# An expert layer with product keys: the first 128 tokens by gathered rows on VectorE, the other 384 by dense blocks summed in six PSUM banks

## The chip, the cores and the metric

The kernel runs on one core of a Trainium2 chip. Times are device microseconds (us) of one launch, 512 tokens of width 1024 in float32. The time before is 4912.36 us, the median of three runs (4911.04 to 4912.63).

## The reference, cut to what matters

The kernel computes the forward pass of two blocks. The first has two mixers and then the layer below, in which each token takes 8 x 16 = 128 of 16384 experts; the second has feed-forward layers and other mixers. The change touches the expert layer alone.

```python
PEER_HEADS = 8; PEER_KEYS = 128; PEER_TOPK = 16; PEER_BLOCK = 128   # D_MODEL = 1024
def peer(h, wq, subkeys, u_tab, v_tab):
    def block(hb):                                          # 128 tokens
        q = (hb @ wq).reshape(PEER_BLOCK, PEER_HEADS, 2, 128)
        s = jnp.einsum('thsd,snd->thsn', q, subkeys)
        s1, i1 = lax.top_k(s[:, :, 0], PEER_TOPK)
        s2, i2 = lax.top_k(s[:, :, 1], PEER_TOPK)
        cand = (s1[..., :, None] + s2[..., None, :]).reshape(PEER_BLOCK, PEER_HEADS, 256)
        sc, ci = lax.top_k(cand, PEER_TOPK)
        e1 = jnp.take_along_axis(i1, ci // PEER_TOPK, axis=-1)
        e2 = jnp.take_along_axis(i2, ci % PEER_TOPK, axis=-1)
        idx = e1 * PEER_KEYS + e2
        gate = jax.nn.softmax(sc, axis=-1)
        act = jax.nn.gelu(jnp.einsum('td,thkd->thk', hb, u_tab[idx])) * gate
        return jnp.einsum('thk,thkd->td', act, v_tab[idx])
```

`u_tab` and `v_tab` are 16384 x 1024, 64 MB each. All matrix products in the kernel are made exact in float32 by three products of halves: an operand x is split as x = H + L (ACT casts H, a second engine subtracts to get L), and one product is HH, HL and LH (`mm3`, L297 to L301).

## The kernel before, in words

The layer works on all experts for all tokens. The tables are cut into 128 blocks of 128 experts (a block has one e1 and all e2). Its three stages follow each other on TensorE:

1. **Queries** (`peer_select`, `dense` with `wq`): q for 512 tokens, scores against the keys (L1098), and the first choice of 16 (L1102 to L1106), in V and I, token-major.
2. **Select**: `routing` is a generator of 156 steps (`STEPS`), and three of them are issued beside each block of U activations of the first `NU` = 56 blocks (`peer_act`). For each of four groups t of 128 tokens, seven steps are `topk` (the choice among 256 pairs, on VectorE; POOL makes the candidates and one multiply, L1187; TensorE transposes the result to `eT`). Then 32 steps build the table of gates: for each token two one-hot tiles of 128 x 128 (the row with the gate on VectorE, L1140; the other on POOL, VectorE or ACT, L1138) and one matmul of them (L1141) into `sa`, copied by ACT to `W`; a block of 32 tokens goes to DRAM as 2 MB (`WD`, 16 of them). The activations of those 56 blocks go to DRAM as `geD`.
3. **Dense**: `peer_dense` takes the blocks in groups of J = 4. 14 groups have their activations in DRAM ("spilled"), 18 make them on the spot ("fresh"); a table `order` mixes the two. For a block: 24 matmuls of U with 512 columns (fresh groups alone; `xH`, `xL` are the activations' names in the trace, `wd` and `we` the weights'), gelu, times the gates (L1233), split into `pGH` and `pGL`, V split into `pVH` and `pVL`, then 8 tiles of 128 channels x 3 matmuls with V stationary and 512 tokens of G moving, into a bank `mm`. After four blocks each of the eight sums is added from PSUM to `pacc` by VectorE (L1256). In the last group the residual r is updated (L1260), the last three channel tiles by halves of the tokens, and the sums of squares for the norm follow it (`Stat`, L2110 to L2149; squares on ACT, their sum on POOL, L2120). The first matmul of the next feed-forward layer (L299 `mm<-xH,weH`) needs that norm.

DMA queues: weights, W, ge and tables all go by SP's queue; POOL issues only a few loads in the stages before. `self.wp` holds the raw weights (`wraw`, two buffers of two blocks each). Pools give a new tile when the last use of the buffer has ended; a scheduler orders each engine's instructions.

Of the kernel before, what the change touches and what calls it, by code (L numbers as in the profile page):

```python
# [9 lines left out]
F32 = mybir.dt.float32  # L10
# [9 lines left out]
T = 512  # L20
# [10 lines left out]
STEPS = 4 * (7 + 32)     # of the routing  # L31
# [48 lines left out]
# the order in which the projections' tiles are taken: per SSD group xs, xs, B, C and z, z;  # L80
# then Hyena's parts v, x1, x2 by slabs of 256 channels, x2 behind by two slabs
# [14 lines left out]
def prep(inp):  # L96
# [33 lines left out]
    # constants that depend on shapes alone  # L130
# [4 lines left out]
    # Hyena  # L135
# [5 lines left out]
    a['pv'] = i['peer_v'][0].reshape(128, 128, 1024)  # L141
# [5 lines left out]
def hy_consts(a, i):  # L147
# [3 lines left out]
    for arg in ((2 * f.T + 1) * (2 * t.T), (2 * f.T + 1) * (2 * t.T + 1), (2 * f + 1) * (2 * t)):  # L151
        # rows (256) on partitions in 2 tiles, columns [cos 256 | sin 256]
# [16 lines left out]
    dec = np.exp(-tt * deltas).astype(f32) * f32(1.0 / 512)     # with the inverse transform's factor  # L169
    # time tiles: even 0,1 then odd 0,1; per slab of 256 channels  # L170
# [4 lines left out]
    # [64][slab][order][dir][256]  # L175
# [21 lines left out]
    # even mixer: qk, v, o, rg_x, rg_g; the gates' inputs apart  # L197
# [23 lines left out]
    # odd mixer: low-rank inputs, then r, k, v by pairs of heads; v, q, k, og of the other  # L221
# [20 lines left out]
    # block of 64, its causal part, and for each level of the inverse the lower left of a pair of blocks  # L242
# [6 lines left out]
# ---------------------------------------------------------------- kernel  # L249
class Kern:  # L250
    def __init__(self, ctx, tc, ap, at, dbg=None):
# [12 lines left out]
        # le: [s, l] s<=l ; ge ; gt ; lt  # L264
# [18 lines left out]
    # PSUM tags: mm (dense), sa, sb (small)  # L283
# [3 lines left out]
    def split(self, pool, x, name, shape=None, bufs=1, l_eng=None):  # L287
        """exact halves of x in float32r: x = H + L"""
# [33 lines left out]
    def wsplit(self, raw, l_eng=None):  # L322
        """halves of weights: every third in xp, where that is open"""
# [13 lines left out]
    def dense_steps(self, src, first, n, kt, movs, evac, chunks=None, g=128, head=0, tail=0, last=None, l_eng=None, early=(0, 0)):  # L337
        """dense, tile by tile"""
# [55 lines left out]
    def softplus(self, pool, x, out, tmpname, p, n):  # L394
        """out = max(x,0) + log1p(exp(-|x|)), by the atanh series"""
# [7 lines left out]
        nc.vector.tensor_mul(e, e, r)            # s = e / (2 + e)  # L403
        nc.vector.tensor_mul(r, e, e)            # s^2
# [15 lines left out]
        # a first guess from the halved exponent, then Newton's steps  # L420
# [7 lines left out]
    def col_bcast(self, out, col, n):  # L428
        """out[m, c*128 + t] = col[t, c] for every m"""
# [14 lines left out]
    def mod_steps(self, *sixths):  # L444
        """sixths of shift1, scale1, gate1, shift2, scale2, gate2, a quarter of one at a step"""
# [44 lines left out]
        # running sums in the chunk, what is left of it, and the whole  # L490
# [30 lines left out]
    def row_bcast(self, dst, src, r, n, rep):  # L521
        """dst[j*rep + i] = src[r + j] for i < rep, j < n (src in DRAM)"""
# [4 lines left out]
    def conv(self, tp, ps, n, taps, bias, name, bufs=3):  # L527
        """centred depthwise convolution of a PSUM tile"""
# [19 lines left out]
    def ssd_states(self, g, tp, R, got, out):  # L548
        """a group's convolved projections -> x times dt, token-major, and the states before each chunk: nine steps"""
# [12 lines left out]
        # both ways through the chunks of the sequence  # L562
# [25 lines left out]
    def ssd_heads(self, g, tp, R, got, xd, S, out):  # L588
        """a group's outputs before the gate -> two tiles; nine steps"""
# [51 lines left out]
    def ssd_gate(self, g, tp, y, z):  # L641
        """group_rmsnorm(y * silu(z))"""
# [19 lines left out]
    def ssd(self, tp, fl, fc, mod):  # L662
# [27 lines left out]
        # a group's heads beside the next one's states, projections between  # L690
# [387 lines left out]
    def peer_select(self, f2):  # L1078
# [5 lines left out]
        with self.tc.tile_pool(name='pk', bufs=1, reuse_waits='tile') as pk:  # L1084
# [31 lines left out]
            for _ in steps:  # L1116
                pass
# [1117 lines left out]
```

## Time and profile before

| what | us |
|---|---|
| median of three runs | 4912.36 |
| span of the profiled execution | 4912.9 |
| its TensorE busy | 4731.6 |
| Select: 1026.0 to 1553.0 | 527.0 |
| Dense: 1553.0 to 2627.0 | 1074.0 |
| last matmul with V to the next layer's first matmul | 6.0 |

The profiled execution's span agrees with the median of the runs within 0.6 us, so differences within the trace can be set against the runs directly. The two stages are 1601 us of it; what lies ahead and behind is not touched, apart from the seam at each end.

### The profile page before, as it was taken

The numbers are of one execution on the slowest core, as the hardware profiler recorded it, in microseconds if no ns is written. First come the engines' busy times: TensorE is split into PE (matmuls) and PEld (weight loads), VectorE is DVE, ScalarE is ACT, GpSimd is POOL, SyncE is SP. The second block draws the span as 40 slices with busy tenths as digits, with TensorE's granted clock in tenths as the row PEclk, the third lists the DMA queues.
The fourth block names the chain that finished last, engine by engine and source line by source line (L and its number), as shares of the span: only waits on it lengthen the run. The fifth ranks groups of instructions, "written<-read, shape, count | busy, mean of one in ns | idle before, by whom it ended". The sixth has DMA issues, their size and how long they took to land.

```text
span 4912.9 us, 60507 instructions
## 1 busy us (share of the span) xinstructions
PE 4731.6 (96%) x23772; PEld 3883.8 (79%) x23772; DVE 2691.2 (55%) x5211; ACT 1736.9 (35%) x2642; POOL 733.5 (15%) x694
## 2 busy tenths in 40 slices
PE   8888999998999999999999999999999999999998
PEld 4776778867888888888888888688888887778887
DVE  5775577699554545555555336663343356645333
ACT  3533222335664222322223225532232233333222
POOL 3232332355441000000001002010020020001001
PEclk9998999999999999999999999999999999998999
DMA  6232423234445444344342222222222220011322
GB/s 213 85 109 94 144 108 125 104 120 151 165 178 184 151 132 146 131 149 150 129 137 86 95 92 78 80 77 95 97 92 95 93 97 8 26 44 44 103 100 72
DMA packets 206873, 537.51 MB, mean 109 GB/s; under 512 B 11555, under 2 KB 79411, under 8 KB 199676
## 3 DMA queue, kind: packets, MB, share of 16 engines
q1 hardware_dynamic: 205084, 526.29, 31.5%
q0 software_dynamic: 1504, 7.34, 0.4%
q8 instruction: 188, 3.08, 0.3%
q14 instruction: 97, 0.79, 0.1%
HBM read 468.50 MB, written 65.09 MB: 109 GB/s over the span
## 4 chain that ended last, share of the span: by engine, by line
PE 72%; issue 13%; DVE 9%; POOL 2%; ACT 2%; DMA 2%; SPq 0%; ACTq 0%; POOLq 0%; DVEq 0%
PE mm L300 20%; PE mm L301 20%; PE mm L299 20%; PE sa L1141 2%; DMA ssee<-csD 2%; DVE oh L1140 1%; PE sa L453 1%; POOL oh L1138 1%; DVE wdL L294 1%; PE sb L2161 0%; PE sa L431 0%; POOL xL L2211 0%; PE sb L1842 0%; PE sa L1842 0%; PE sb L1849 0%
## 5 line engine op out<-in xcount | busy, mean ns | idle before, releaser
L299 PE MATMUL mm<-xH,wdH 128*128 128x512 f32 (+2 forms) x2660 | 1019.3, 385 | 9.4 <-DVE cacc L539 7.8
L301 PE MATMUL mm<-xH,wdL 128*128 128x512 f32 (+2 forms) x2660 | 1014.0, 382 | 7.4 <-DVE wdL L294 7.2
L300 PE MATMUL mm<-xL,wdH 128*128 128x512 f32 (+2 forms) x2660 | 1015.7, 382 | 2.7 <-POOL xL L2211 1.5
L293 ACT CAST wdH<-wraw 128x1024 fp32r<-128x1024 f32 (+2 forms) x382 | 394.6, 1035 | 1165.9 <-PE mm L300 833.3
L294 DVE TENSOR_TENSOR wdL<-wraw,wdH 128x1024 fp32r<-128x1024 f32 (+2 forms) x346 | 424.3, 1226 | 457.1 <-ACT wdH L293 444.4
L299 PEld LDWEIGHTS mm<-xH,wdH 128*128 128x128 f32 (+1 forms) x2660 | 505.8, 191 | 106.2 <-issue 12.5
L301 PEld LDWEIGHTS mm<-xH,wdL 128*128 128x128 f32 (+1 forms) x2660 | 506.9, 191 | 102.7 <-DVE wdL L294 10.2
L300 PEld LDWEIGHTS mm<-xL,wdH 128*128 128x128 f32 (+1 forms) x2660 | 507.0, 191 | 95.9 <-POOL xL L2211 3.3
L299 PE MATMUL mm<-xH,weH 128*128 128x512 f32 (+2 forms) x1048 | 400.7, 382 | 1.1 <-ACT xH L2209 1.1
L300 PE MATMUL mm<-pGL,pVH 128*128 128x512 f32 (+1 forms) x1036 | 401.4, 390 | 0.0
L300 PE MATMUL mm<-xL,weH 128*128 128x512 f32 (+2 forms) x1048 | 399.4, 381 | 1.0 <-POOL xL L2211 0.9
L299 PE MATMUL mm<-pGH,pVH 128*128 128x512 f32 (+1 forms) x1036 | 399.3, 387 | 0.0
L301 PE MATMUL mm<-pGH,pVL 128*128 128x512 f32 (+1 forms) x1036 | 399.3, 388 | 0.0
L301 PE MATMUL mm<-xH,weL 128*128 128x512 f32 (+2 forms) x1048 | 397.1, 379 | 0.4 <-POOL weL L294 0.3
L293 ACT CAST weH<-wraw 128x1024 fp32r<-128x1024 f32 (+2 forms) x162 | 168.2, 1038 | 469.4 <-PE mm L300 327.8
L294 DVE TENSOR_TENSOR weL<-wraw,weH 128x1024 fp32r<-128x1024 f32 (+1 forms) x155 | 190.0, 1226 | 230.9 <-ACT weH L293 205.2
L293 ACT CAST pVH<-wraw 128x1024 fp32r<-128x1024 f32 x128 | 133.0, 1052 | 486.6 <-PE mm L300 295.4
L1256 DVE TENSOR_TENSOR pacc<-pacc,mm 128x512 f32<-128x512 f32 (+1 forms) x251 | 166.7, 678 | 179.5 <-PE mm L301 179.2
L294 DVE TENSOR_TENSOR pVL<-wraw,pVH 128x1024 fp32r<-128x1024 f32 x128 | 155.2, 1223 | 179.6 <-ACT pVH L293 179.5
L300 PEld LDWEIGHTS mm<-pGL,pVH 128*128 128x128 f32 x1036 | 195.2, 188 | 44.4 <-DVE pGL L294 6.3
L299 PEld LDWEIGHTS mm<-xH,weH 128*128 128x128 f32 (+1 forms) x1048 | 198.4, 189 | 39.0 <-issue 1.4
L300 PEld LDWEIGHTS mm<-xL,weH 128*128 128x128 f32 (+1 forms) x1048 | 197.9, 189 | 38.4 <-POOL xL L2211 2.0
(1203 smaller groups left out, 8402.9 us busy)
## 6 DMA issues: line engine op xcount, KB each, us to landing
wraw<-in_wi_dram SPq DMA_DIRECT2D x88, 1024.0 KB, 4.9
wraw<-in_pv_dram SPq DMA_DIRECT2D x64, 1024.0 KB, 5.0
wraw<-in_pu_dram SPq DMA_DIRECT2D x63, 1024.0 KB, 5.1
WD<-W SPq DMA_DIRECT2D x16, 2048.0 KB, 8.1
pW<-WD SPq DMA_DIRECT2D x32, 1024.0 KB, 5.7
wraw<-in_wmod_dram SPq DMA_DIRECT2D x24, 1024.0 KB, 7.3
wraw<-in_win_dram SPq DMA_DIRECT2D x24, 1024.0 KB, 5.1
wraw<-in_wo_dram SPq DMA_DIRECT2D x16, 1024.0 KB, 4.9
```

The source lines that it names most:

```text
L293: nc.scalar.copy(h, x)
L294: (l_eng or nc.vector).tensor_sub(l, x, h.bitcast(F32))
L299: mm(out, wh, xh, start=start, stop=False)
L300: mm(out, wh, xl, start=False, stop=False)
L301: mm(out, wl, xh, start=False, stop=stop)
L453: nc.tensor.matmul(pr[0:2, 0:256], self.silc[:, k], raw[:, k // 4, w], start=k == 0, stop=k == 7)
L1138: (nc.gpsimd, nc.vector)[i // 2].tensor_scalar(o2[:, i], io, e2, None, op0=OP.is_equal)
L1140: nc.vector.tensor_scalar(o1, io, eT[:, 0, c0 + i:c0 + i + 1], eT[:, 2, c0 + i:c0 + i + 1], op0=OP.is_equal, op1=OP.mult)
L1141: nc.tensor.matmul(ps[:, i * 128:i * 128 + 128], o2[:, i], o1, start=True, stop=True)
L1256: nc.vector.tensor_add(acc[:, d, half], acc[:, d, half], ps)
```

## The change

- **Host layout**: a third input `pun`, U untransposed (row = expert), is passed; `pv` becomes 16384 rows of 1024.
- **The first 128 tokens** (`peer_own`): their activations are brought token-major into `pfh` (16 fp32 matmuls with the identity). `topk` of t = 0 leaves indices in `pfI` and gates in `pfG`, both token-major, and makes no one-hot tiles. A generator `own` then has 256 steps. Each works on one tile `pfr`, 128 rows x 1024 fetched by an indirect DMA from POOL's queue (a row of the table for each token, 512 KB): 128 steps multiply a row of `pun` with `pfh` and sum it (`tensor_tensor_reduce`), 128 steps add a row of `pv` times its activation to `pfo`. Four buffers `pfr` (`AHEAD`); the next fetch into a buffer is issued behind the step that reads it. Steps go 16 U, 16 U, 16 V, 16 U, ... so that gelu and gates are taken for 16 at a time. In the code one step is asked for beside each of the last 53 of the 56 blocks of the select stage, and one or two beside each block of the dense stage; the scheduler may move them.
- **The other 384 tokens** (`TD`): U with 384 moving columns instead of 512; 12 blocks of one-hot work instead of 16; `topk` of t = 1 follows that of t = 0 at once.
- **The product with V**: G (128 experts x 128 tokens) is now stationary and V moves with 512 channels: 3 token tiles x 2 halves x 3 = 18 matmuls a block, summed over all 128 blocks in six PSUM banks (four `mm`, two `sa`); U goes into `sb`. `pacc` and its additions are gone. `pG` has three buffers, `pV` two, V's raw tiles their own two (`praw`).
- **The end**: six copies from PSUM, 32 fp32 transposes of 128 x 128 (three token tiles and `pfo`, for eight channel tiles), then the update of r and `Stat`, on whole tiles of 512 tokens.

The diff's core; comments are removed all over the file, which shifts line numbers:

```diff
+TD = T - 128
+STEPS = 7 + 3 * (7 + 32)
+AHEAD = 4
...
-    a['pv'] = i['peer_v'][0].reshape(128, 128, 1024)
+    a['pv'] = i['peer_v'][0]
+    a['pun'] = i['peer_u'][0]
...
+    def peer_own(self, tp, f2):
+        f = tp.tile([128, 1024], F32, name='pfh')
+        for h in range(2):
+            ps = self.mmps(('sa', 'sb')[h], 2)
+            for k in range(4):
+                for q in range(2):
+                    nc.tensor.matmul(ps[:, k * 128:k * 128 + 128], f2[q][:, 4 * h + k, 0:128].bitcast(F32), self.ident, start=q == 0, stop=q == 1)
+            nc.scalar.copy(f[:, 512 * h:512 * h + 512], ps)
...
+        yield
+        todo = []
+        for g in range(9):
+            todo += [('pun', 16 * g + i) for i in range(16) if g < 8]
+            todo += [('pv', 16 * g - 16 + i) for i in range(16) if g > 0]
...
+                row = tp.tile([128, 1024], F32, name='pfr', bufs=AHEAD)
+                nc.gpsimd.indirect_dma_start(out=row, out_offset=None, in_=ap[n], in_offset=bass.IndirectOffsetOnAxis(ap=self.ownI[:, k:k + 1], axis=0))
...
+        for i, (n, k) in enumerate(todo):
+            row = rows[i]
+            if n == 'pun':
+                nc.vector.tensor_tensor_reduce(row, row, f, 1.0, 0.0, OP.mult, OP.add, dots[:, k:k + 1])
+                if k % 16 == 15:
+                    d = dots[:, k - 15:k + 1]
+                    nc.scalar.activation(d, d, AF.Gelu)
+                    nc.vector.tensor_mul(d, d, self.ownG[:, k - 15:k + 1])
+            elif k == 0:
+                nc.vector.tensor_scalar(self.own, row, dots[:, 0:1], None, op0=OP.mult)
+            else:
+                nc.vector.scalar_tensor_tensor(self.own, row, dots[:, k:k + 1], self.own, op0=OP.mult, op1=OP.add)
+            fetch(i + AHEAD)
+            yield
...
             for b, ge in self.peer_act(pk, f2, 0, NU, 3):
...
+                    n += 1
+                if n > 9:
+                    next(own)
...
-            for b in range(4 * t, 4 * t + 4):
+            for b in range(4 * t - 4, 4 * t):
+                if t == 0:
+                    break
...
+        if t == 0:
+            nc.vector.scalar_tensor_tensor(self.ownI, res[:, 0], 128.0, res[:, 1], op0=OP.mult, op1=OP.add)
+            yield
+            return
...
-                self.mm3(ps, uh[:, s], ul[:, s], f2[0][:, k], f2[1][:, k], k == 0, k == 7)
+                self.mm3(ps, uh[:, s], ul[:, s], f2[0][:, k, 128:T], f2[1][:, k, 128:T], k == 0, k == 7)
...
-            def product(ps, d, half, js):
-                s = slice(d * 128, d * 128 + 128)
-                for j in js:
-                    self.mm3(ps, Vh[j][0][:, s], Vh[j][1][:, s], G[j][0][:, half], G[j][1][:, half], j == 0, j == J - 1)
...
-                    nc.vector.tensor_add(acc[:, d, half], acc[:, d, half], ps)
...
+        acc = [[self.mmps() for _ in range(2)] for _ in range(2)] + [[self.mmps('sa', 2) for _ in range(2)]]
+        G, Vh = acts(), values()
+        nxt = next(G)
+        for i in range(128):
+            (gh, gl), (vh, vl) = nxt, next(Vh)
+            nxt = next(G, None)
+
+            for t, h in ([(t, h) for t in range(3) for h in range(2)] if i < 127 else [(t, h) for h in range(2) for t in range(3)]):
+                s, c = slice(t * 128, t * 128 + 128), slice(h * 512, h * 512 + 512)
+                self.mm3(acc[t][h], gh[:, s], gl[:, s], vh[:, c], vl[:, c], i == 0, i == 127)
+            for _ in range(2 if i % 5 < 3 else 1):
+                next(own, None)
...
+            for d in range(4 * h, 4 * h + 4):
+                ps = self.mmps('sb', 2)
+                for t in range(4):
+                    nc.tensor.transpose(ps[:, t * 128:t * 128 + 128], o[t][:, d * 128:d * 128 + 128], self.ident)
+                nc.vector.scalar_tensor_tensor(r[:, d], ps, self.M[:, 40 + d, 0:1], r[:, d], op0=OP.mult, op1=OP.add)
+                st.tile(d)
```

What the scheduler makes of it on VectorE in the select stage, before: one-hot tiles (`oh`) for four tokens, a split of U (`wdL`), one-hot tiles again.

```order
L1138 TENSOR_SCALAR oh_11144<-iota,eT 128x128
L1138 TENSOR_SCALAR oh_11164<-iota,eT 128x128
L294 TENSOR_TENSOR wdL<-wraw,wdH 128x1024
L1140 TENSOR_SCALAR oh_11146<-iota,eT 128x128
L1140 TENSOR_SCALAR oh_11150<-iota,eT 128x128
```

The same place of the changed kernel (L1198 and L1196 are the one-hot tiles' new lines, L1118 the product with a fetched row).

```order
L1118 ISA pfr,pfD<-pfr,pfh 128x1024
L1118 ISA pfD 128x1
L297 TENSOR_TENSOR wdL<-wraw,wdH 128x1024
L1198 TENSOR_SCALAR oh_9068<-iota,eT 128x128
L1198 TENSOR_SCALAR oh_9072<-iota,eT 128x128
```

A `tensor_tensor_reduce` has become two instructions, a main one and one that writes its 128 sums; 53 of these pairs and 32 steps with V rows stand ahead of the dense stage's first split of G, and the one-hot tiles there on VectorE go from 640 to 480.

VectorE in the dense stage, before (`pge` times gates, `pacc` sums, splits of V and G):

```order
L1233 TENSOR_TENSOR pge<-pge,pW 128x512
L1256 TENSOR_TENSOR pacc<-pacc,mm 128x512 x4
L294 TENSOR_TENSOR pVL<-wraw,pVH 128x1024
L294 TENSOR_TENSOR pGL<-pge,pGH 128x512
L1256 TENSOR_TENSOR pacc<-pacc,mm 128x512
L294 TENSOR_TENSOR pGL<-pge,pGH 128x512 x2
```

And after (`pfo` sums the fetched V rows):

```order
L1126 SCALAR_TENSOR_TENSOR pfo<-pfr,pfD,pfo 128x1024 x3
L1296 TENSOR_TENSOR pge<-pge,pW 128x384
L297 TENSOR_TENSOR weL<-wraw,weH 128x1024
L297 TENSOR_TENSOR pGL<-pge,pGH 128x384
L1126 SCALAR_TENSOR_TENSOR pfo<-pfr,pfD,pfo 128x1024
L1296 TENSOR_TENSOR pge<-pge,pW 128x384
L297 TENSOR_TENSOR pVL<-praw,pVH 128x1024
```

The `pacc` rows are gone; 171 steps of `own` (96 with V rows, 75 with U rows) stand between the splits that feed TensorE.

POOL in the dense stage issued nothing before; now its order there is the gathers alone, each behind the VectorE step that frees its buffer:

```order
L1110 DMA pfr<-in_pv_dram,pfI 128x1024 x3
L1110 DMA pfr<-in_pun_dram,pfI 128x1024 x16
L1110 DMA pfr<-in_pv_dram,pfI 128x1024 x16
L1110 DMA pfr<-in_pun_dram,pfI 128x1024 x16
```

They alternate by 16 as the steps do, and in the select stage they stand between POOL's one-hot tiles.

## Rows read from the trace of the kernel before

**Rows 1.** Windows by stage: length, then busy time (instructions) of each engine.

```profile
core 0: us, PE busy (x) PEld busy (x) DVE busy (x) ACT busy (x) POOL busy (x), PEclk, DMA share, GB/s
1026.00:1553.00 527.00, 493.29 (x2549) 408.55 (x2549) 368.69 (x1009) 296.98 (x531) 244.41 (x298) 0.97 0.45 165
1553.00:2627.00 1074.00, 1072.41 (x4749) 884.58 (x4748) 560.65 (x707) 316.01 (x406) 8.71 (x8) 1.00 0.42 139
```

**Rows 2.** Timeline of PE, the dense stage: start, duration, matmuls of 512 columns.

```profile
1700.12 0.39 PE L299 MATMUL mm<-pGH,pVH 128*128 128x512 f32 x1
...
1701.03 0.39 PE L300 MATMUL mm<-pGL,pVH 128*128 128x512 f32 x1
```

**Rows 3.** Timeline of PE, the next layer's first tiles: matmuls of 256 columns.

```profile
2649.73 0.28 PE L299 MATMUL mm<-xH,wdH 128*128 128x256 f32 x1
...
2651.77 0.28 PE L301 MATMUL mm<-xH,wdL 128*128 128x256 f32 x1
```

**Rows 4.** Timeline of PE, one-hot matmuls, eight to a row.

```profile
1202.16 1.06 PE L1141 MATMUL sa<-oh,oh 128*128 128x128 f32 x8
...
1203.29 1.05 PE L1141 MATMUL sa<-oh,oh 128*128 128x128 f32 x8
```

**Rows 5.** Lines of VectorE, select: count, busy us, mean ns, idle before, releaser.

```profile
L1140 DVE TENSOR_SCALAR oh<-iota,eT 128x128 f32<-128x128 f32 x512 | 168.4, 392 | 95.9 <-PE sa L1141 94.6
L294 DVE TENSOR_TENSOR wdL<-wraw,wdH 128x1024 fp32r<-128x1024 f32 x38 | 47.8, 1257 | 33.4 <-ACT wdH L293 33.4
L1138 DVE TENSOR_SCALAR oh<-iota,eT 128x128 f32<-128x128 f32 x128 | 34.3, 298 | 0.0
L294 DVE TENSOR_TENSOR weL<-wraw,weH 128x1024 fp32r<-128x1024 f32 x19 | 23.5, 1237 | 16.3 <-ACT weH L293 16.3
L1185 DVE TENSOR_TENSOR tkeq<-tkabf,iota 128x1024 f32<-128x1024 f32 x16 | 22.7, 1426 | 0.0
L1188 DVE TENSOR_REDUCE tkr<-tkeq 128x64 f32<-128x1024 f32 x16 | 19.2, 1204 | 5.6 <-POOL tkeq L1187 5.6
```

**Rows 6.** Lines of VectorE, dense, 1560 to 2600, shapes kept apart.

```profile
L1256 DVE TENSOR_TENSOR pacc<-pacc,mm 128x512 f32<-128x512 f32 x240 | 160.8, 684 | 171.9 <-PE mm L301 171.6
L294 DVE TENSOR_TENSOR pVL<-wraw,pVH 128x1024 fp32r<-128x1024 f32 x123 | 149.2, 1223 | 175.9 <-ACT pVH L293 175.9
L294 DVE TENSOR_TENSOR pGL<-pge,pGH 128x512 fp32r<-128x512 f32 x122 | 82.8, 689 | 33.4 <-ACT pGH L293 32.3
L1233 DVE TENSOR_TENSOR pge<-pge,pW 128x512 f32<-128x512 f32 x121 | 82.2, 688 | 75.0 <-ACT pge L1207 62.7 <-DMA pge<-geD 12.3
```

**Rows 7.** One line each on VectorE: ns min/median/max, first and last start, forms.

```profile
L1260 DVE SCALAR_TENSOR_TENSOR r<-pacc,modM,r x11: 485/743/1665, 2608.6 to 2627.6; 128x256 f32<-128x256 f32 x6, 128x512 f32<-128x512 f32 x5
...
L2164 DVE COPY ns<-sb x18: 151/166/167, 118.2 to 4896.7; 128x8 f32<-128x8 f32 x13, 128x4 f32<-128x4 f32 x5
```

**Rows 8.** DMA by queue: packets, MB, share of 16 engines' span.

```profile
q1 hardware_dynamic: 205084, 526.29, 31.5%
```

**Rows 9.** DMA issues: count, KB each, median us from issue to landing.

```profile
wraw<-in_pv_dram SPq DMA_DIRECT2D x64, 1024.0 KB, 5.0
...
wraw<-in_wo_dram SPq DMA_DIRECT2D x32, 512.0 KB, 3.8
...
dftL<-in_dftL_dram POOLq DMA_DIRECT2D x1, 512.0 KB, 13.8
```

**Rows 10.** One line on POOL: ns min/median/max of a DMA's issue.

```profile
L1052 POOL DMA_DIRECT2D wor<-oD x8: 536/562/598, 823.7 to 861.1; - x8
```

**Rows 11.** Timeline of POOL and VectorE, select: a choice among pairs meets one-hot tiles.

```profile
1210.78 5.56 POOL L1187 TENSOR_TENSOR tkeq<-tkeq,tkIf 128x1024 f32<-128x1024 f32 x2 [3.39 <-DVE tkeq L1185]
...
1211.74 4.68 DVE L1140 TENSOR_SCALAR oh<-iota,eT 128x128 f32<-128x128 f32 x2
```

**Rows 12.** Timeline of the end of the layer.

```profile
2613.26 2.66 POOL L2120 TENSOR_TENSOR nqa<-nqa,nsq 128x512 f32<-128x512 f32 x2 [0.74 <-ACT nsq L2115]
...
2626.61 0.28 PE L301 MATMUL mm<-pGH,pVL 128*128 128x256 f32 x1
...
2632.58 0.58 PE L299 MATMUL mm<-xH,weH 128*128 128x256 f32 x1 [1.09 <-ACT xH L2209]
```

More of the change, by code (lines that the diff above doesn't have):

```diff
@@ L1071, in phase_b @@
             f2 = st.halves(xp, gain, self.M[:, 24:32, 0])
-        self.peer_select(f2)
-        with self.tc.tile_pool(name='pd', bufs=1, reuse_waits='tile') as pd:
-            st = Stat(self, pd, r, 1e-6, False)
-            self.peer_dense(pd, f2, r, st)
-            return st.halves(xp, self.v('final_norm'), None, True, 4.0 ** 0.25)
-    def peer_select(self, f2):
+        with self.tc.tile_pool(name='pf', bufs=1, reuse_waits='tile') as pf:
+            own = self.peer_own(pf, f2)
+            next(own)
+            self.peer_select(f2, own)
+            with self.tc.tile_pool(name='pd', bufs=1, reuse_waits='tile') as pd:
+                st = Stat(self, pd, r, 1e-6, False)
+                self.peer_dense(pd, f2, r, st, own)
+                return st.halves(xp, self.v('final_norm'), None, True, 4.0 ** 0.25)
@@ new lines, in peer_own, with fetch @@
+    def peer_own(self, tp, f2):
+        nc, ap = self.nc, self.ap
+        f = tp.tile([128, 1024], F32, name='pfh')
[5 more added lines that the diff above has]
+            nc.scalar.copy(f[:, 512 * h:512 * h + 512], ps)
+        self.ownI = tp.tile([128, 128], U32, name='pfI')
+        self.ownG = tp.tile([128, 128], F32, name='pfG')
+        dots = tp.tile([128, 128], F32, name='pfD')
+        self.own = tp.tile([128, 1024], F32, name='pfo')
+        yield
[3 more added lines that the diff above has]
+            todo += [('pv', 16 * g - 16 + i) for i in range(16) if g > 0]
+        rows = []
+        def fetch(i):
+            if i < len(todo):
+                n, k = todo[i]
+                row = tp.tile([128, 1024], F32, name='pfr', bufs=AHEAD)
+                nc.gpsimd.indirect_dma_start(out=row, out_offset=None, in_=ap[n], in_offset=bass.IndirectOffsetOnAxis(ap=self.ownI[:, k:k + 1], axis=0))
+                rows.append(row)
+        for i in range(AHEAD):
+            fetch(i)
+        for i, (n, k) in enumerate(todo):
[12 more added lines that the diff above has]
+            yield
@@ L1081, in peer_select @@
+    def peer_select(self, f2, own):
         nc, tc, ap = self.nc, self.tc, self.ap
         mov = [(T, lambda k: f2[0][:, k], lambda k: f2[1][:, k])]
-        self.geD = self.dram.tile([NU, 128, T], F32, name='geD')
+        self.geD = self.dram.tile([NU, 128, TD], F32, name='geD')
         with self.tc.tile_pool(name='pk', bufs=1, reuse_waits='tile') as pk:
@@ L1109, in peer_select @@
             steps = self.routing(pk, V, I, eT, io)
+            n = 0
             for b, ge in self.peer_act(pk, f2, 0, NU, 3):
@@ L1115, in peer_select @@
                     next(steps, None)
+                    n += 1
+                if n > 9:
+                    next(own)
             for _ in steps:
@@ L1192, in topk, with peer_act @@
             nc.tensor.transpose(ps[:, q * 128:q * 128 + 128], res[:, q], self.ident)
-        nc.scalar.copy(eT[:, :, t * 128:t * 128 + 128], ps[:, 0:384].rearrange('p (q t) -> p q t', q=3))
+        nc.scalar.copy(eT[:, :, t * 128 - 128:t * 128], ps[:, 0:384].rearrange('p (q t) -> p q t', q=3))
         yield
-    def peer_act(self, tp, f2, first, n, pool=0):
+    def peer_act(self, tp, f2, first, n, pool=0, tag=('mm', 4)):
         nc = self.nc
         us = chain(self.weights(self.ap['pu'], first, pool, 1024, l_eng=nc.gpsimd), self.weights(self.ap['pu'], first + pool, n - pool, 1024))
+        w = next(us)
@@ L1200, in peer_act @@
         for b in range(first, first + n):
-            uh, ul = next(us)
-            ps = self.mmps()
+            uh, ul = w
+            ps = self.mmps(*tag)[:, 0:TD]
             for k in range(8):
                 s = slice(k * 128, k * 128 + 128)
-                self.mm3(ps, uh[:, s], ul[:, s], f2[0][:, k], f2[1][:, k], k == 0, k == 7)
-            ge = tp.tile([128, T], F32, name='pge', bufs=3)
+                self.mm3(ps, uh[:, s], ul[:, s], f2[0][:, k, 128:T], f2[1][:, k, 128:T], k == 0, k == 7)
@@ new lines, in peer_dense, with spilled, acts @@
+        fresh = self.peer_act(pd, f2, NU, 128 - NU, tag=('sb', 2))
+        def spilled(grp):
+            for b in range(J * grp, J * grp + J):
+                ge = pd.tile([128, TD], F32, name='pge', bufs=3)
+                nc.sync.dma_start(ge, self.geD[b])
+                yield b, ge
+        def acts():
+            for grp in order:
+                W = pd.tile([128, 12, J, 32], F32, name='pW', bufs=2)
+                nc.sync.dma_start(W, self.WD[:, :, J * grp:J * grp + J, :])
+                for b, ge in spilled(grp) if J * grp < NU else islice(fresh, J):
+                    gv = ge.rearrange('p (a b) -> p a b', a=12)
+                    nc.vector.tensor_mul(gv, gv, W[:, :, b % J])
+                    yield self.split(pd, ge, 'pG', bufs=3)
@@ new lines, in values @@
+        def values():
+            for grp in order:
+                for i in range(0, J, 2):
+                    raw = pd.tile([128, 2, 1024], F32, name='praw', bufs=2)
+                    nc.sync.dma_start(raw, ap['pv'][128 * (J * grp + i):128 * (J * grp + i + 2)].rearrange('(t p) f -> p t f', t=2))
+                    for q in range(2):
+                        yield self.split(pd, raw[:, q], 'pV', bufs=2)
+        acc = [[self.mmps() for _ in range(2)] for _ in range(2)] + [[self.mmps('sa', 2) for _ in range(2)]]
@@ new lines, in peer_dense @@
+        for _ in own:
+            pass
+        o = [self.own] + [pd.tile([128, 1024], F32, name=f'po{t}') for t in range(3)]
+        for h in range(2):
+            c = slice(h * 512, h * 512 + 512)
+            for t in range(3):
+                (nc.scalar.copy, nc.vector.tensor_copy)[t % 2](o[t + 1][:, c], acc[t][h])
+            for d in range(4 * h, 4 * h + 4):
[4 more added lines that the diff above has]
+                st.tile(d)
```

59 lines of the change are left out of this document (11 added, 48 removed).

## The prediction, made before the changed kernel was run

> **What bounds the kernel now.** I read the windows by stage first [rows 1]. The reader is to see that TensorE (PE) is busy 1072 of the 1074 us of the dense stage, at a granted clock of 1.00, while VectorE is busy half of it and the DMA engines 0.42 of it. In the select stage PE is busy 493 of 527 us, VectorE 369. So in both a matmul less is time less, until another engine comes up. Then I read the pace of the matmuls in the timeline, not their listed durations, which overlap. From 1700.12 to 1701.03 lie four steps of 512 columns: 0.227 us each [rows 2]. With 256 columns 17 steps take 2649.73 to 2651.77: 0.120 us each [rows 3]. A matmul of a one-hot pair takes (1203.29 - 1202.16) / 8 = 0.14 us, and every one of them stands twice in the trace, 1024 for 512 tokens [rows 4]. Last come VectorE's lines in both stages [rows 5, 6], because this change hands it work.
>
> **PE's work, part by part.**
> - V: 3072 matmuls of 512 columns (128 blocks x 24) become 2304 (128 x 18) of the same length, with G in place of V as the stationary operand. 768 x 0.227 = -174 us.
> - U: 3072 matmuls go from 512 to 384 columns. No row shows 384. The two paces lie on a line of 0.107 us for 256 columns, so 384 take (0.227 + 0.120) / 2 = 0.1735 us. Bounds: 0.120 (256 columns' pace) and 0.227 (no gain). I take the middle because the pace at 256 columns is already near half, so the weight load between matmuls doesn't set it. 3072 x 0.0535 = -164 us.
> - One-hot: 4 of 16 blocks go, 256 records x 0.14 = -36 us.
> - Added: 16 fp32 matmuls of the token-major copy ahead of the stage, recorded twice, 32 x 0.14 = 4.5 us on the path; 32 transposes at the end, below.
>
> So PE loses about 370 us. The question is how much of it comes through.
>
> **Select stage (527 us).** The order puts 1419 U matmuls ahead of the first with V (17 blocks of them behind the last one-hot tile). PE: 1419 x 0.1735 + 768 x 0.14 + 15 for transposes and modulation = 369 us. VectorE: 368.7 before; 160 one-hot tiles less at (168.4 + 34.3) / 640 = 0.317 us give -51 [rows 5]; added are 53 products with U rows and 32 sums with V rows. No row shows the product with a sum. The plain product or difference of 128x1024 takes 1.22 us [rows 6], a copy of a few columns, as the second of its instructions, 0.166 [rows 7]: 1.39 together. The sum with a V row is a SCALAR_TENSOR_TENSOR with two SBUF inputs; its two forms took 485 ns at the least for 256 and 743 in the middle for 512 columns, 1.0 ns an element more, so 1.26 us for 1024 [rows 7]. 53 x 1.39 + 32 x 1.26 = +114. VectorE then has 432 us of work, PE 369: VectorE becomes the engine that is full. Before, the fuller engine had 493 of 527, 34 us of waiting; now choices on VectorE and one-hot work follow each other less evenly, so I add 43 and take 475 us. Bounds: 432 (no waiting) and 527 (all gained on PE is lost). Saved: 52. POOL is busy 244 us there [rows 1], loses a quarter of its one-hot tiles and gets 85 issues at about 0.56 us [rows 10], so it is not the limit.
>
> **Dense stage (1074 us).** PE: 2304 x 0.227 + 1653 x 0.1735 = 523 + 287 = 810 us. VectorE for each block: pVL 1.22, the gates and pGL at three quarters 0.52 + 0.52; on the whole 128 x 2.26 + 70 splits of U at 1.22 + 75 x 1.39 + 96 x 1.26 = 600 us. Gone are the 240 sums into pacc, 161 us [rows 6], so VectorE's total hardly changes. DMA: before, 526.29 MB took 31.5% of 16 engines' 4912.9 us, 340 GB/s when all are busy [rows 8]. Each block now needs 0.52 MB of V, 0.2 of gates, 0.2 or 0.52 for the activations, and 1.34 gathers of 0.52 MB: about 1.8 MB, 231 MB in all, 680 us of 810. Both fit on average, but not everywhere: runs of blocks with spilled activations need PE for only 18 x 0.227 = 4.09 us a block, and VectorE for 2.26 + 1.6 own steps of 1.33 = 4.4, DMA for 5 at that rate. The buffers hold a few blocks. 56 such blocks x 0.4 gives 25 us; bounds are nothing (the buffers cover it) and 56 x 0.9 = 50. I take 810 + 25 = 835. Saved: 239.
>
> What is queued behind a step that waits: VectorE's queue is in order, so a product whose rows have not landed holds the splits pGL and pVL that PE waits for. Four fetches ahead at a step each 3 to 6 us leave 12 us or more for one to land; 512 KB landed in 3.8 us from SP's queue and in 13.8 at the worst on POOL's, four loads of 3 MB together [rows 9]. I count this wait as nothing, and it is the cover whose loss the third case prices.
>
> **The end.** Before, the last matmul with V stands at 2626.61, the next layer's first at 2632.58, 6.0 us [rows 12], since the last tiles went by halves. Now six copies, 32 transposes (recorded twice, 64 x 0.14 = 9), the updates of r, and then squares summed on POOL at 2.66 / 2 = 1.33 us a tile [rows 12]: eight tiles make a chain of about 10 us, half of it beside the last matmuls' second half, then the norm for four token tiles. I add 15 us; bounds 5 and 22.
>
> **Sum.** -52 - 239 + 15 + 4.5 = -272. The trace's span is 4912.9, its runs' median 0.6 lower: 4641, say 4640 us. Own range with the bounds (select -95 to 0, dense -264 to -214, end +5 to +22): 4563 to 4725, most of it 4600 to 4690.
>
> **Rivals.**
> *The product with a sum runs at half rate.* [...] For it: nothing here shows the instruction. Against: the SCALAR_TENSOR_TENSOR with two SBUF inputs kept 1.0 ns an element [rows 7]. Price: select is VectorE's, 53 x 1.23 = +65; in dense 75 x 1.23 = 92 us more on an engine with 600 of 835; I let a fifth of it through, where spilled runs leave no room: +18. 4640 + 83 = 4723. [...]
>
> *A gather's work on POOL holds VectorE* (slower side). Place: every step's next fetch is issued beside VectorE's two-input splits. For it: at 1210.78 a multiply on POOL and VectorE's one-hot tiles run into each other, 4.68 us for two tiles that otherwise take 0.4 each [rows 5, 11]. Against: the POOL DMA issues of before took 0.56 us and are 8 [rows 10]. If each gather takes g us from VectorE, select has 475 + 85 g, dense 128 x (4.7 + 1.34 g) once that passes 835, that is from g = 1.4. With 600 for VectorE's own work in dense and 20 for the seams it is slower than before from 475 + 600 + 20 + 256 g > 1601, g = 2.0 us. At g = 5.56 / 2 = 2.78, as long as one of those multiplies [rows 11], it gives 475 + 600 + 20 + 256 x 2.78 = 1807, 206 more: 5118. [...]
>
> *The gathers themselves set the pace.* 171 of them in dense at a period p: 171 p passes 835 at p = 4.9 us. 512 KB at 340 GB/s are 1.5 us, the median load of 512 KB took 3.8 from issue to landing with others in flight [rows 9]; four in flight hide that. At p = 5.5 dense takes 940 and select, 85 gathers in the later two thirds, 500: 4770. At 13.8 us alone, with four in flight, p is 3.5, and nothing is lost.
>
> *384 columns cost as much as 512.* The gain on U's 164 goes: 4640 + 92 in dense, little in select: 4740. The pace of 256 columns speaks against it [rows 3].
>
> **How the numbers follow.** My forecast 0.60, half rate 0.16, gathers' pace 0.10, 384 columns 0.03, some other loss that leaves it under before (0.02), VectorE held beyond 2 us 0.07, no change within 0.2% (10 us, about what can be told from none here) 0.02. Faster by more than that 0.91, same 0.02, slower 0.07. The range that leaves out two in ten: 4590 to 4775, which takes in the half-rate and most of the third case, and leaves the slow one out.
>
> **What would show it.** Steps of 0.17 us between U matmuls; V matmuls still 0.227; no sums of pacc. Product with a sum near 1.2 us and not 2.4. In select VectorE at 0.9 busy and PE waiting for one-hot tiles; in dense PE near full at 835 us, its waits for pVL and pGL in the spilled runs; DMA share near 0.8. Last V matmul to the next layer about 21 us. It is wrong if VectorE waits for `pfr` (gathers late), if its splits stretch beside POOL's gathers, or if PE waits as much as it lost.

## The result and the profile after

The changed kernel takes 4732.7 us (median of four runs, 4729.8 to 4733.7) against 4911.7 for the kernel before beside it: a ratio of 0.9639, 95% interval 0.9627 to 0.9652, so 3.6% faster. The forecast was 4640 us in a range of 4590 to 4775: the sign and the range held, but of the 272 us forecast 179 came, and the range held by luck (below). The profiled execution (4730.2 us) shows where the rest stayed. The stages are cut at the last score matmul of the queries, the first and the last matmul with V, and the next layer's first matmul; all in us:

| stage | before | after | forecast | saved |
|---|---|---|---|---|
| select | 526.7 | 472.9 | 475 | 53.8 |
| dense | 1073.8 | 929.3 | 835 | 144.5 |
| seam | 6.0 | 21.6 | 21 | -15.6 |
| all else | 3306.4 | 3306.4 | +4.5 | 0 |

Select and seam came as forecast; the dense stage is 94 us too long, and that is the whole miss. The 4.5 us forecast for the token-major copy do not show: all else takes as long as before. The windows of the changed kernel (columns as in [rows 1]): its two stages, then three pieces of the dense one.

```profile
1024.00:1497.00 473.00, 390.84 (x2267) 359.60 (x2265) 408.35 (x986) 243.06 (x430) 349.64 (x324) 0.91 0.70 254
1497.00:2427.00 930.00, 855.29 (x3958) 734.87 (x3959) 567.47 (x701) 293.14 (x402) 215.95 (x167) 0.96 0.70 244
...
1600.00:1700.00 100.00, 85.42 (x374) 71.62 (x373) 75.34 (x98) 25.75 (x36) 47.52 (x38) 0.92 0.89 320
...
1970.00:2100.00 130.00, 130.00 (x640) 115.89 (x639) 59.97 (x73) 47.49 (x64) 0.00 (x0) 1.00 0.50 168
2100.00:2427.00 327.00, 325.35 (x1582) 287.45 (x1581) 144.48 (x176) 116.30 (x156) 0.00 (x0) 1.00 0.47 159
```

The reader is to see two kernels in one stage. Until 1970 the DMA engines are busy 0.9 of the time at 320 GB/s, and PE stands still a seventh of it; from 1970 on POOL has no gather left, the DMA share is 0.5, and PE is full. The average of the whole stage, 0.70, is not far from what I had forecast ("near 0.8") and says nothing of either half. The gathers stand on POOL's lines (ns min/median/max, first and last start):

```profile
L1110 POOL DMA_INDIRECT pfr<-in_pun_dram,pfI x128: 932/1048/1990, 1052.2 to 1868.5; - x128
L1110 POOL DMA_INDIRECT pfr<-in_pv_dram,pfI x128: 932/1064/2072, 1314.1 to 1960.0; - x128
```

All 256 are issued by 1960. VectorE took 170 of their steps in the stretch from 1497 to 1970, beside the splits of 59 blocks: 2.9 a block, where the code asks for 1.6 and I had spread 171 over 128 blocks, 1.34 each. What VectorE waited for in that stretch, and PE up to 2000 (us in total, times, longest), then ACT's copies of V in the stretch (count, busy us, mean ns, idle before):

```profile
DVE pfo L1126 <- DMA pfr<-in_pv_dram,pfI: 40.0, 29, 3.3
DVE pge L1296 <- DMA pge<-geD: 33.6, 15, 5.4
DVE pfr L1118 <- DMA pfr<-in_pun_dram,pfI: 30.9, 28, 2.6
```

```profile
PE mm L302 <- ACT pGH L296: 47.2, 20, 5.7
PE mm L303 <- DVE pVL L297: 14.8, 8, 3.9
PE mm L304 <- DVE pGL L297: 10.4, 16, 2.3
PE mm L302 <- ACT pVH L296: 9.4, 1, 9.4
```

```profile
L296 ACT CAST pVH<-praw 128x1024 fp32r<-128x1024 f32 x60 | 62.7, 1047 | 46.1 <-PE sa L304 43.5 <-DMA praw<-in_pv_dram 2.5
```

VectorE's queue stands 105 us for data, and the splits behind it reach PE late: 82 us of waits, the longest of them, 9.4 us, ahead of the first matmul with V. Of VectorE's 105 us 71 are for the gathered rows themselves and 34 for loaded activations; V's raw tiles kept ACT only 2.5 us, and the gates don't appear. At the rates of [rows 2, 3] the stretch holds 1047 x 0.227 + 698 x 0.1735 = 359 us of matmuls; it took 473. Of the 114 lost 73 are idle time of PE (400 of 473 busy) and 41 pass while PE is busy. Most of these are the clock (some 26 us, an estimate from the rows below): in this stretch its granted share, recorded as 0.5 or 1.0 and nothing between, falls to 0.5 thirteen times for 3.4 to 6.8 us, 67 us together, and from 1970 on it is 1.00. What PE did before and in such a stretch, from 1526.8 to 1530.2, stands in its timeline:

```profile
1523.57 0.50 PE L302 MATMUL mm<-pVH,pGH 128*128 128x512 f32 x1 [0.98 <-ACT pGH L296]
1526.38 0.50 PE L304 MATMUL mm<-pVH,pGL 128*128 128x512 f32 x1 [2.08 <-DVE pGL L297]
...
1527.07 0.63 PE L303 MATMUL mm<-pVL,pGH 128*128 128x512 f32 x1
...
1529.63 0.63 PE L303 MATMUL mm<-pVL,pGH 128*128 128x512 f32 x1
```

It waited twice in 3 us; then six steps take 2.56 us, 0.427 each for 0.227. PE was busy for some 55 of the 67 us at the lower clock, so about 26 us went there. Each of the thirteen falls begins in or right behind a wait of PE of 1.8 to 5.7 us; five other waits, of 2.1 to 2.7 us, passed without one. So a late load could be paid for twice here, in the wait and in the clock behind it.

The durations I had bounded, VectorE's lines of the changed kernel from 1020 to 2560 (as [rows 6]):

```profile
L1126 DVE SCALAR_TENSOR_TENSOR pfo<-pfr,pfD,pfo 128x1024 f32<-128x1024 f32 x127 | 163.1, 1284 | 59.6 <-DMA pfr<-in_pv_dram,pfI 58.8
L297 DVE TENSOR_TENSOR pVL<-praw,pVH 128x1024 fp32r<-128x1024 f32 x128 | 156.5, 1223 | 98.7 <-ACT pVH L296 98.6
L1118 DVE CUSTOM_DVE_ANT_0 pfr<-pfr,pfh 128x1024 f32<-128x1024 f32 x128 | 155.1, 1223 | 46.3 <-DMA pfr<-in_pun_dram,pfI 46.0
...
L1118 DVE DVE_READ_ACCUMULATOR2_ANT pfD<- 128x1 f32 x128 | 10.6, 83 | 0.0
```

The product with a sum takes 1.223 + 0.083 us (I took 1.39), the sum with a V row 1.284 (1.26). The split of V keeps the 1223 ns of [rows 6] beside POOL's gathers. And PE's pace at 384 columns, and at 512 with G stationary:

```profile
1026.06 0.34 PE L304 MATMUL mm<-xH,wdL 128*128 128x384 f32 x1
...
1027.10 0.34 PE L304 MATMUL mm<-xH,wdL 128*128 128x384 f32 x1
...
1514.65 0.39 PE L302 MATMUL sa<-pVH,pGH 128*128 128x512 f32 x1
...
1515.56 0.39 PE L303 MATMUL sa<-pVL,pGH 128*128 128x512 f32 x1
```

Six steps in 1.04 us: 0.173 each, as the line between [rows 2] and [rows 3] gave. Four steps of 512 columns in 0.91 us: 0.227 each, as before.

### The profile page after: what moved, and what is told of

Its sections match the earlier page's. It is cut to its first block, busy times and chain, and to the rows that moved or that the text cites. A ratio compares the mean times of both kernels' runs of the same rounds, so it can differ in the third digit from the quotient of the medians.

```text
span 4730.2 us, 58670 instructions
## 1 busy us (share of the span) xinstructions
PE 4421.4 (93%) x22773; PEld 3694.3 (78%) x22773; DVE 2740.6 (58%) x5167; ACT 1665.1 (35%) x2540; POOL 1053.6 (22%) x880
## 3 DMA queue, kind: packets, MB, share of 16 engines
q0 software_dynamic: 38368, 141.58, 8.2%
## 5 line engine op out<-in xcount | busy, mean ns | idle before, releaser
L304 PE MATMUL mm<-xH,wdL 128*128 128x512 f32 (+4 forms) x2276 | 849.4, 374 | 19.2 <-DVE wdL L297 18.9
L302 PE MATMUL mm<-xH,wdH 128*128 128x512 f32 (+4 forms) x2276 | 852.9, 377 | 8.3 <-DVE cacc L542 8.3
L303 PE MATMUL mm<-xL,wdH 128*128 128x512 f32 (+4 forms) x2276 | 848.6, 374 | 2.7 <-POOL xL L2282 1.5
L304 PEld LDWEIGHTS mm<-xH,wdL 128*128 128x128 f32 (+2 forms) x2276 | 434.0, 191 | 90.9 <-DVE wdL L297 25.1
L302 PEld LDWEIGHTS mm<-xH,wdH 128*128 128x128 f32 (+2 forms) x2276 | 434.0, 192 | 78.6 <-issue 13.4
L303 PEld LDWEIGHTS mm<-xL,wdH 128*128 128x128 f32 (+2 forms) x2276 | 435.1, 191 | 70.5 <-POOL xL L2282 3.3
L302 PE MATMUL mm<-pVH,pGH 128*128 128x512 f32 x512 | 210.9, 413 | 56.6 <-ACT pGH L296 47.2
L303 PE MATMUL mm<-pVL,pGH 128*128 128x512 f32 x512 | 210.9, 412 | 16.5 <-DVE pVL L297 16.4
L304 PE MATMUL mm<-pVH,pGL 128*128 128x512 f32 x512 | 212.4, 415 | 10.6 <-DVE pGL L297 10.4
L297 DVE TENSOR_TENSOR pVL<-praw,pVH 128x1024 fp32r<-128x1024 f32 x128 | 156.5, 1223 | 98.7 <-ACT pVH L296 98.6
L1110 POOL DMA_INDIRECT pfr<-in_pun_dram,pfI x128 | 165.9, 1296 | 164.2 <-DVE pfD L1118 96.5
```

Source lines behind the costliest of these rows:

```text
L297: (l_eng or nc.vector).tensor_sub(l, x, h.bitcast(F32))
L302: mm(out, wh, xh, start=start, stop=False)
L303: mm(out, wh, xl, start=False, stop=False)
L304: mm(out, wl, xh, start=False, stop=stop)
L1110: nc.gpsimd.indirect_dma_start(out=row, out_offset=None, in_=ap[n], in_offset=bass.IndirectOffsetOnAxis(ap=self.ownI[:, k:k + 1], axis=0))
```

## Experiments

Theory 1: the gathers come bunched, fill the DMA engines for half of the stage, and the loads of V, gates and activations land late (by the waits above: activations and the rows themselves). Theory 2: the steps' own time on VectorE, in whose queue the splits stand. Theory 3: each gather's work on POOL holds other work, wherever it stands. Stage times below are cut as in the first table.

**The steps paced by block.**

```diff
+            at = self.cut.ins              # the split of V of block i on VectorE
             nxt = next(G, None)
...
             for _ in range(2 if i % 5 < 3 else 1):
-                next(own, None)
+                with self.tc.issue_after(at):
+                    next(own, None)
```

> The changed kernel with one thing added: each of the first tokens' steps in the dense stage is queued on VectorE behind the split of V of its block, so that they come at 1.6 a block over all 128 blocks, instead of 3 a block until block 59. All work is the same. Theory 1 (the bunched gathers fill the DMA engines, and the loads of V, gates and activations come late): the dense stage, 929 us in the changed kernel, falls to 835 to 855, DMA share near 0.7 throughout, total 4640 to 4665. Theory 2 (the steps' own time on VectorE, in whose queue the splits stand): a gain too, but less, 20 to 50 us. Theory 3 (each gather's work on POOL holds VectorE or the splits wherever it stands): no gain, total about 4730.

Measured: 4623.0 us (4613.9 to 4628.3), ratio 0.9419 (0.9404 to 0.9435), 2.3% less than the changed kernel, from the order alone. Dense 849.1, select 437.4 (53 steps stand there now, not 86), seam 21.6. The dense stage and a piece of it:

```profile
1460.00:2310.00 850.00, 830.90 (x3968) 726.57 (x3967) 609.44 (x754) 299.08 (x403) 274.46 (x199) 0.99 0.81 286
1500.00:1700.00 200.00, 194.44 (x937) 170.94 (x936) 142.05 (x172) 69.57 (x93) 65.22 (x47) 0.99 0.83 291
```

More gathers lie in the stage than before (203 for 170), and PE is busy 831 of 850. Theory 3 falls. The DMA share is 0.8 and not 0.7, since more gathers moved into the stage. The dense stage is in the range expected; the total is under it, since select fell by 35 us as well, which I had not expected.

**Three steps a block again.** In the code above `range(2 if i % 5 < 3 else 1)` becomes `range(3)`.

> As the paced kernel, but with 3 steps queued behind each block's split of V instead of 1.6, until they are used up at block 68. All work is the same; only the pace goes back to the changed kernel's. Theory 1 (bunched gathers fill the DMA engines): 68 blocks need about 173 MB, 530 us at 325 GB/s, against 430 us of TensorE: dense back to 910 to 940 us, select as in the paced kernel (437), total 4685 to 4720. Rival (it was not the pace but something else that the queueing changed, such as the 86 steps ahead of the dense stage): dense stays near 850, total near 4625.

Measured: 4686.3 us, 0.9541 (0.9522 to 0.9560); dense 916.3, select 441.0. The pace alone costs 67 us in the dense stage: it is the pace, not the queueing. Both times are in the ranges of theory 1. From 1600 to 1800 the DMA share is 0.95, PE busy 176 of 200:

```profile
1600.00:1800.00 200.00, 176.37 (x786) 146.61 (x786) 161.96 (x209) 57.97 (x80) 98.81 (x77) 0.96 0.95 343
```

**VectorE's steps without the gathers, and the gathers without the steps.** The first at 3 a block:

```diff
-                row = tp.tile([128, 1024], F32, name='pfr', bufs=AHEAD)
-                nc.gpsimd.indirect_dma_start(out=row, ...)
+                if i < 3:
+                    row = tp.tile([128, 1024], F32, name=f'pfr{i}')
+                    nc.gpsimd.indirect_dma_start(out=row, ...)
...
+                else:
+                    rows.append(rows[i - 3])
```

> Steps at 3 a block as the changed kernel has them, but only three tiles of rows are fetched, and all 256 steps work on these (products go to a tile of their own): the gathers' transfers and POOL's work are gone, VectorE's work is all there. Sums are of the wrong rows. Theory 1: dense 815 to 840 us, total near 4630. Theory 2: dense stays near 900 to 930, total 4700 or more. Theory 3: as theory 1.

Measured: 4570.0 us, 0.9308 (0.9289 to 0.9326), dense 815.9. From 1500 to 1700:

```profile
1500.00:1700.00 200.00, 200.00 (x978) 177.57 (x977) 198.12 (x257) 74.19 (x100) 0.00 (x0) 1.00 0.52 178
```

VectorE is busy 198 of 200 us and PE 200 of 200. The steps' time is there in full and costs the dense stage nothing; theory 2 falls. (The total is 60 us under what I expected, since select takes 422.6.)

The other half, in the scheduler's order:

```diff
-                nc.vector.tensor_tensor_reduce(row, row, f, 1.0, 0.0, OP.mult, OP.add, dots[:, k:k + 1])
+                nc.vector.tensor_scalar(dots, row[:, 0:128], self.ownG[:, k:k + 1], None, op0=OP.mult)
```

(and the sum with V rows in the same way).

> All 256 gathers stay, but VectorE's step on each is cut to 128 of 1024 columns (a scaled copy, some 0.3 us in place of 1.3), in the scheduler's own order. The sums for the first 128 tokens are left out. Theory 1: bunched as much or more, dense 900 to 940 us, DMA share 0.9 while the gathers last. Theory 2: dense near 830. Theory 3: dense as long as in the changed kernel.

Measured: 4746.4 us, 0.9667 (0.9648 to 0.9686): with VectorE relieved, slower than the changed kernel. The dense stage takes 914.7 us, as theory 1 had it and not 830, but 15 less than in the changed kernel; the loss is in select, 497.4 for 472.9, where 119 gathers now stand instead of 89. Buffers come free sooner, the gathers bunch more (over by 1846), and in the dense stage the DMA engines have no room while they last (select, then the dense stage up to there):

```profile
1030.00:1527.00 497.00, 393.07 (x2254) 365.96 (x2252) 343.20 (x962) 238.69 (x431) 340.44 (x353) 0.91 0.74 271
1527.00:1846.00 319.00, 255.92 (x1085) 213.60 (x1086) 135.61 (x265) 79.88 (x113) 153.62 (x136) 0.90 0.96 349
```

**Neither.** `for g in range(9)` becomes `range(0)`, so that no step and no gather is left.

> The first 128 tokens' steps are left out whole (no gathers, no steps, zeros for their sums); the other 384 tokens as in the changed kernel. All theories: the floor of the change: dense 812 to 822 us by TensorE alone, select 430 to 460, total 4590 to 4630. What lies between this and the changed kernel is the price of the first tokens' path.

Measured: 4554.4 us, 0.9276 (0.9257 to 0.9295); dense 815.6, select 407.5. The dense stage's floor is PE's alone (busy 814.4 of 815.0 us, at a clock of 1.00): I had put 810 for it. Select and total are under what I expected. The first tokens' path costs 178 us in the changed kernel and 69 when it is paced, 30 of these in select.

**Half of the gathers' cost, two ways.** At 3 a block, so that it stands against 4686 us. First, half of the rows:

```diff
-out=row, ... ap=self.ownI[:, k:k + 1]
+out=row[0:64], ... ap=self.ownI[0:64, k:k + 1]
```

> Three steps a block as in the run with 3, but each gather fetches the rows of 64 of the 128 tokens and each step works on those 64 partitions; the sums of the other 64 tokens are left out. As many gathers, as many POOL and VectorE instructions of the same columns, half the bytes. Theory 1: 68 blocks need 128 MB, 395 us at 325 GB/s, under TensorE's 430: dense 820 to 850, total 4590 to 4630. Rival (the number of gathers counts: POOL's time for each, four buffers and the way until a gather has landed): dense as in the run with 3 full gathers, 900 or more.

Measured: 4722.0 us, 0.9614 (0.9594 to 0.9633); dense 960.6: slower with half the bytes. The rival's "900 or more" came, but 44 us above the run with 3 full gathers is more than it says. The software queue's line on the page of that run, then of this one (packets, MB, share of 16 engines), and this one's window from 1600 to 1800:

```profile
q0 software_dynamic: 38368, 141.58, 8.2%
```

```profile
q0 software_dynamic: 21984, 74.47, 6.3%
```

```profile
1600.00:1800.00 200.00, 166.04 (x720) 138.55 (x720) 150.81 (x189) 53.31 (x74) 111.97 (x72) 0.91 0.84 223
```

Half the bytes took three quarters of the engines' time (6.3% for 8.2), so it was no halving; a packet of 4096 bytes had 288 ns in the middle from 1500 to 1950, against 159 in the other run, and packets of other loads grew too (1536 bytes: 65 to 100). Why packets into 64 partitions take longer, no run shows. VectorE waited 126 us for its rows here, 77 in the run with 3, at a DMA share of 0.84 in place of 0.95 from 1600 to 1800: the lower mean share of the 16 engines went with the longer waits. The run doesn't decide between bytes and number. So half of the columns for all rows:

```diff
-row = tp.tile([128, 1024], ...); in_=ap[n]
+row = tp.tile([128, 512], ...); in_=ap[n].rearrange('e (h d) -> (e h) d', h=2)
...
-            row = rows[i]
+            row = rows[i][:, None, :].to_broadcast([128, 2, 512])
```

> Three steps a block, as in the run with 3; each gather brings all 128 tokens' rows, but 512 of 1024 columns, and VectorE's step reads them twice, so its 1024 columns and the number of gathers, POOL instructions and packets stay. The sums of the first 128 tokens are wrong. It halves what the gathers cost the DMA engines without narrowing the destination to 64 partitions, where a packet of 4096 bytes had taken 288 ns in the middle instead of 159. Theory 1 (DMA engines' time): gathers' packets near 86 ns as those of 2048 bytes before, DMA share under 0.8, dense 820 to 850, total 4590 to 4630. Rival (the number of gathers counts, through POOL, four buffers and the way until one has landed): dense 900 or more, total 4680 or more.

Measured: 4618.1 us, 0.9402 (0.9383 to 0.9421), dense 851.4, just outside what I wrote. Its queue line, and 1600 to 1800:

```profile
q0 software_dynamic: 21984, 74.47, 4.8%
```

```profile
1600.00:1800.00 200.00, 188.98 (x895) 162.67 (x894) 184.53 (x243) 66.33 (x93) 123.08 (x87) 0.99 0.80 276
```

As many gathers, issued as tightly, with VectorE busier than in the run with 3 (184.5 for 162.0): 65 us less in the dense stage. The packets did not stay, as I had expected, but halved in number (21984 for 38368), at 4096 bytes and 159 ns each. What counts is what the gathers lay on the DMA engines, not how many gathers there are; whether bytes or packets is not told apart.

**Pace by kind of block, and more buffers.**

```diff
-            for _ in range(2 if i % 5 < 3 else 1):
+            due += (9, 41)[J * order[i // J] >= NU]
+            k, due = due // 16, due % 16
+            for _ in range(k):
```

> As the paced kernel, but the steps go where TensorE has more to do: 2.56 behind a block that makes its activations (about 8.25 us of TensorE), 0.56 behind one whose activations are loaded (4.1 us). Theory 1: then 309 and 280 GB/s are wanted in the two kinds in place of about 260 and 400, and the paced kernel's remaining 33 us over the floor of 816 shrink: dense 822 to 842, total 4595 to 4618. Rival (what is left is the gathers' work on POOL beside VectorE, whatever the place): no change from 4623.

Measured: 4657.9 us, 0.9485 (0.9470 to 0.9501): 35 us worse than the even pace; dense 884.2. A miss for both sides: the sum of bytes for each kind of block, each by itself, doesn't forecast this. VectorE's wait for loaded activations had grown (41.3 us at the even pace), which the next two runs take up:

```profile
DVE pge L1296 <- DMA pge<-geD: 79.7, 36, 7.1
```

> The paced kernel with six buffers in place of three for the activations in the dense stage, so that those that wait in DRAM can be loaded further ahead. In the paced kernel VectorE waited 41 us for these loads and the dense stage is 33 us over the floor. If what is left is the loads' lateness: dense 825 to 842, total 4600 to 4616. If it is not (the splits of V are late, which have two buffers): no change from 4623.

> The run by kind (2.56 steps behind a block that makes its activations, 0.56 behind one that loads them; 4658 us, where I expected a gain) with the same six buffers. If it lost to the even pace because the loads of activations come late behind the gathers of the blocks ahead (VectorE waited 80 us for them, 41 at the even pace): total back to 4600 to 4630. If not: 4650 to 4660.

Measured, with `bufs=6` for `pge` in the dense stage: 4627.3 us, 0.9421 (0.9405 to 0.9437) at the even pace; 4664.7, 0.9500 (0.9484 to 0.9515) by kind. No change in either, and VectorE's waits for these loads stayed (42.5 and 72.7 us), so the number of these buffers is not it. At the even pace SP's queue, which issues them, stood 298 us for V's raw buffers; whether the loads of activations wait their turn behind these was not tested. Why the pace by kind loses to the even one stays open, as do the even pace's last 33 us over the floor.

**The end by halves.**

```diff
+        for at in last:
+            product([0], at)               # blocks 126 and 127, tokens 128 to 255
+        take(0)
+        product([1, 2], last[0])
+        update(0)                          # r and squares of tokens 0 to 255
+        product([1, 2], last[1])
```

> The run by kind, and at the end the last two blocks' products are taken for tokens 128 to 255 first, so that the update of r and the sums for the norm of tokens 0 to 255 lie beside the rest, and the norm goes by halves of the tokens. The seam of 21.6 us between the last matmul with V and the next layer should fall to 8 to 14 us: total 8 to 13 us below the run by kind. Against it: the chain of sums on POOL gets twice as many instructions of half the length, and the first half's ends may wait for PSUM banks: no gain.

Measured: 4656.3 us, 0.9481 (0.9466 to 0.9497), beside 4657.9 for the run by kind. The seam fell from 21.6 to 14.7 us, the dense stage grew by 5, and the total is 1.5 us lower where I expected 8 to 13: a miss. With the even pace:

> The even pace of 1.6 steps a block with the end by halves of the tokens. If the end's gain of some 5 us that the run by kind and halves shows in its seam is real and the even pace is the better one: 4612 to 4622, against 4623 for the paced kernel; if the halves take elsewhere what they give at the seam, 4623.

Measured: 4619.4 us (4602.3 to 4627.0), 0.9410 (0.9394 to 0.9425); seam 14.6. It can't be told from the paced kernel's 0.9419. Both beat the kernel before and the changed one.

## Why the prediction held, and the step that failed

- **The range** held by luck. My own bounds gave 4563 to 4725, and 4733 is outside. The stated range reached 4775 for the half rate and for slow gathers, and neither came as described. One of its signs of being wrong did show: VectorE waited for `pfr`.
- **PE's terms** held: 0.173 us for 384 columns, 0.227 for 512 with G stationary, and the floor without the first tokens is 816 us where the sum said 810.
- **Select** came at 473 for 475, but the two parts of the sum were off against each other. I took VectorE for 432 us of work and 43 of waiting; it was busy 408 and idle 65, 34 of these for gathered rows. PE, busy 391 at a clock of 0.91, waited longest for the choices among pairs on VectorE (`tkr`: 31 us, line below). Steps there were 86, as counted (85); with 53, paced, it is 437. What else sets the stage is not shown.
- **The failed step** is the DMA sum of the dense stage: "Each block now needs ... 1.34 gathers ... about 1.8 MB, 231 MB in all, 680 us of 810. Both fit on average, but not everywhere". The bytes were right (930 us at 244 GB/s are 227 MB). The average was not the state of any block: 2.9 gathers stood in each of the first 59, none in the last 69. The 25 us for places that don't fit, and 50 as the bound, should have been 119 (929 - 810). I had looked for such places in the spilled runs and taken the steps' even spacing from the code; the order of the instructions was the place to count them. At the 1.6 steps a block that the code asks for, the dense stage took 849, 14 us over the forecast's 835; the whole came 17 under 4640, since select fell too.
- **The wait put at nothing** is one way in which the loss reached PE, and the second failed step: "a product whose rows have not landed holds the splits" was right (up to 1578.21 VectorE stood 2.50 us for a row; the split `wdL`, whose `wdH` ACT had made by 1571.92, started behind it at 1579.84), "I count this wait as nothing" was not. VectorE stood 71 us for rows in the stretch. Four fetches ahead were to leave 12 us at a step each 3 to 6; steps came every 2.8 us, which leaves 11, and rows took 7.4 us in the middle and 12.6 at the most to land. How much of the loss is this wait and how much the late activations, no run separates.
- **The half-rate rival** is out: no run shows the 1.23 us more an instruction that its price is added up from. The product with a sum took 1.223 + 0.083 us, the sum with a V row, which also has two SBUF sources, 1.284, a plain difference 1.223.
- **VectorE held by POOL** is out: its splits kept 1223 ns, and 1.0 to 1.3 us of POOL for a gather are under the 2.0 from which I had it slower. The tiles stretched at 1210.78 [rows 11] were TENSOR_SCALAR with one input tile, not the two-input kind that I set beside them.
- **Gathers that set the pace** by being slow (4.9 us each) is out in that form: they came every 473 / 170 = 2.8 us. It was their haste that cost, which no rival of mine had.
- **The seam** came as summed, 21.6 for 21: the chain on POOL stands behind the update of r.

```profile
PE sb L1254 <- DVE tkr L1246: 31.1, 6, 7.3
```

```profile
2427.59 5.92 DVE L1331 SCALAR_TENSOR_TENSOR r<-sb,modM,r 128x512 f32<-128x512 f32 x8 [0.43 <-PE sb L1330]
...
2431.76 6.63 POOL L2191 TENSOR_TENSOR nqa<-nqa,nsq 128x512 f32<-128x512 f32 x5 [0.74 <-ACT nsq L2186]
...
2448.30 0.58 PE L302 MATMUL mm<-xH,weH 128*128 128x256 f32 x1 [1.57 <-ACT xH L2280]
```

## What to carry to other kernels

A transfer that fits on average must also be spread: here the work that was ready early and needed nothing else was taken as fast as its four buffers allowed, 2.9 steps a block in place of 1.6, and it filled the DMA engines (a share of 0.90 at 323 GB/s) until its own transfers and the loads beside it came late (71 and 34 us of waits of VectorE), and the full engine waited behind both (82 us). Before a forecast, count in each engine's order how many such steps stand between two of the steps that matter, and read the DMA share in pieces of the stage, not over it. If it is 0.9 in one half and 0.5 in the other, tie the side work to the main work's blocks: here that gave 110 us for a few lines.

## What the runs showed of the hardware

A gather of 128 rows of 4 KB occupied POOL for 0.93 us at the least and 1.05 in the middle (in the changed kernel; POOL's spans are rough). Into 64 partitions its packets took 288 ns instead of 159, and other loads' packets of 1536 bytes 100 instead of 65. Over stretches of 200 us and more the DMA engines gave at most 343 to 349 GB/s at a share of 0.95 to 0.96, near the 340 worked out from [rows 8]; whether the engines or the memory behind them set this, no run tests. At a share of 0.90 (323 GB/s) PE lost 114 us in 473; at 0.81 (286 GB/s) the dense stage was 33 us over its floor. VectorE, busy 0.99 of its time for 200 us, did not slow PE at all while its data were there (PE busy 200.00 of 200 us).
